# Attention heads in pairs, with products that alternate between halves of the TensorE array

## The chip, the cores and the metric

The kernel runs on one core of one Trainium2 chip. The metric is the device time of one launch in microseconds (us), as the median of several runs. TensorE (PE in the profile) multiplies, VectorE (DVE) and ScalarE (ACT) work on tiles in the two on-chip memories, SBUF and PSUM, GpSimd (POOL) does a few small things, and SyncE (SP) issues the loads.

## The reference, cut to what matters

256 tokens of width 1024 go through two layers of one kind (feed forward, mixer, feed forward) and one block of another (attention, mixture of 32 experts). Attention occurs twice.

- In the mixer of layer 0 there are 4 heads. A head has two queries and two keys of 64 rows each, and values of 128. It subtracts one softmax from the other: `w = probs(qa, k1) - lam * probs(qb, k2)`, and the output is `w @ v`.
- In the last block there are two attentions side by side, each of 8 heads with values of 64 columns. In one (here: moba; with 256 tokens its blocks reduce to plain causal attention) queries and keys have 64 rows, in the other (mla) 64 + 32 = 96.

In each, a score is `q @ k` in 32 bits, scaled and masked causally, and the softmax is taken over the keys.

## The kernel before

Activations lie transposed, features on the 128 partitions and 256 tokens along the columns. Most products are with weights that are split into two float32r parts (`split`: ScalarE's cast on L215, VectorE's subtraction on L216), and three products (`mm3`, L222 to L224) make one full one. Weights come in granules of 1 MB through slots; SyncE's loads are in the order of the program (`dma`, L191), and each waits until its slot is free. The products of attention are plain float32; in the profile such a product is two records of a weight load and a matmul.

A head of attention is a generator, `head` in `mixer0` and `attend` for the last block, with a `yield` between its stages. Stage one: for the first 128 and the last 128 queries (`tt`), the product of queries and keys (128 or 256 columns; L670, L818) into one PSUM bank from the pool `acc` of four, and behind it a bfloat16 product that adds the mask (L672, L819); then VectorE's maxima, ScalarE's exponentials with their sums, VectorE's reciprocal and scaling (L823 to L839). Stage two: three transposes into PSUM (pool `gu` of three; L843) and ScalarE's copy (L845). Stage three: the products with the values (L851 for 256 columns, L852 for 128). Their outputs have 64 partitions, and the halves of a PSUM bank (pool `mi` of one) are filled by an even head and the odd head after it; the odd one also copies the bank out (L855).

`pipeline` lets one head enter a tick; a tick runs one stage of each head under way, the oldest first, and then `n` steps of a generator of fillers. In the last block the fillers are the up projections of mla (six steps for the queries, two for keys and values), eight gates of two steps each, and two parts of an output projection. A step of a projection is 24 `mm3` products. The 16 heads of the last block go through with n = 1, moba's eight first; the four heads of `mixer0` with n = 2. The framework's scheduler orders the instructions of each engine when the program is built, so the order on the chip isn't that of the code in every place; on the chip each engine works strictly through its own list.

Behind the last block's attention come the rest of the output projections and the experts, whose 96 granules are loaded by `moe_fetch` into slots as these come free; the first of these loads are issued during attention.

A product that has no more than 64 rows or 64 output columns is put on a part of the array that follows from the partitions on which its operands and its output start. `gemv_mm` (L266) makes use of that: four products in turn, each writing 32 partitions of one bank.

Of the kernel before, what the change touches and what calls it, by code (L numbers as in the profile page):

```python
# [44 lines left out]
class K:  # L45
# [82 lines left out]
    def pair(self, src0, src1, xH, xL, n, ready=None, inner=True):  # L128
        """Two granules of 256 columns: four PSUM tiles [128, n], side by side (inner) or one after the other."""
# [13 lines left out]
    def gap_fin(self, n, ps):  # L143
        """The product with h, as a tile and a column to be added to it."""
# [23 lines left out]
    def set_ring(self, raw, wsp):  # L168
        """Slots that raw granules and split granules go through, in turn."""
# [19 lines left out]
    def dma(self, dst, src):  # L189
        """Loads are issued in the order of the program."""  # L190
# [4 lines left out]
    def after(self, b, a):  # L195
        """Keeps b behind a in the order of their engine."""
# [4 lines left out]
    def split(self, src, nk, n):  # L201
        """Loads [128, nk*n] and splits it exactly into two float32r parts."""
# [39 lines left out]
    def rows_to_col(self, ps, l, i):  # L242
        """Rows 0, 32, 64, 96 of ps [128, 256] are the quarters of the vector: its columns, plus the bias."""
# [14 lines left out]
    def gemv_mm(self, l, i, ps):  # L258
        """Quarters of c_act @ w_ada[l][:, i] in rows 0, 32, 64, 96 of ps; a granule a step."""
# [16 lines left out]
    def gemv_steps(self, l, i, res):  # L276
        """The same with the products on the vector engine; a granule a step."""
# [24 lines left out]
    def first_cols(self, i, q, col):  # L302
        """Columns 2q, 2q+1 of vector i of layer 0, from the granule of its 256 columns."""
# [24 lines left out]
    def sq_add(self, src, stat):  # L328
        """Takes the squares of src [128, 512] into stat."""
# [6 lines left out]
    def sq_sum(self, stat, lo, hi):  # L336
        """Column sums of pieces lo to hi, [128, 256] each, in four column groups of the array."""
# [22 lines left out]
    def col_sum(self, stat):  # L360
        """Sums over partitions and pieces: [128 tokens, 2] in PSUM."""
# [10 lines left out]
    def bcast(self, rcol, ps=None):  # L372
        """[128 tokens, 2] -> [128, 256] rows, in PSUM."""
# [11 lines left out]
    def h_chunk(self, k, h, rb, a, b, pool=False):  # L385
        """Chunk k of h = x * rstd * a + b, split."""
# [12 lines left out]
    def split_act(self, src, oH, oL):  # L399
        """Splits an SBUF tile."""  # L400
# [4 lines left out]
    def add_res(self, d, srcs, g, stat, nxt=None):  # L405
        """x[2d:2d+2] += g * srcs (PSUM); squares are summed."""
# [13 lines left out]
    def ffn(self, l, j, n, steps, count, ready=None):  # L420
        """n: the operands of gap_begin and gap_end, or h alone with ready, which makes two chunks of h at a time;
        steps: a generator that is advanced once a pair."""
# [72 lines left out]
    def proj_pieces(self, src, nk, cols, xH, xL, evac):  # L495
        """Weights [nk*128, cols] (cols a multiple of 128, up to 256): [128, cols/128, 256] transposed, in PSUM,
        given to evac; a step for each 128 columns."""
# [16 lines left out]
    def tok_pieces(self, src, nk, cols, xH, xL, evac):  # L514
        """Token-major: [128 tokens, 2, cols] in PSUM, given to evac; cols up to 256."""
# [17 lines left out]
    def outproj(self, name, nk, x, g, order=None, nxt=None, then=None):  # L533
        """x(k): the parts of chunk k."""
# [23 lines left out]
    def mixer0(self, n, filler, steps, res):  # L558
# [11 lines left out]
        # statistics over the 64 rows of each component: columns (tt, head, comp)  # L570
# [40 lines left out]
        # lambda  # L611
# [9 lines left out]
        # keys: times rstd over each component  # L621
# [40 lines left out]
        def head(hd):  # L662
            sc = []
            for c in range(2):
                s = self.acc()
                rows = slice(64 * c, 64 * c + 64)
                for tt in range(2):
                    n = P * (tt + 1)
                    o = P * tt
                    nc.tensor.matmul(s[:, o:o + n], qg[rows, hd, tt * P:tt * P + P], kr[rows, hd, :n],  # L670
                                     start=(tt == 0), stop=False, skip_group_check=True)
                    nc.tensor.matmul(s[:, o + n - P:o + n], self.identb, self.maskb,  # L672
                                     start=False, stop=True, skip_group_check=True)
                sc.append(s)
# [25 lines left out]
            # [keys 0, 256 queries | keys 1, 128 queries]  # L700
# [42 lines left out]
    def pipeline(heads, fill, n=1):  # L743
        """Heads enter one a tick; a tick runs one stage of each head under way, the oldest first, and n fillers."""
# [65 lines left out]
    def attend(self, hd, q, k, scol, sconst, vt, out, state):  # L810
        """q, k: [K, 256] slices; scol: [128, 2] query scales or None."""
        nc = self.nc
        s = self.acc()
        offs = (0, P)
        for tt in range(2):
            n = P * (tt + 1)
            o = offs[tt]
            nc.tensor.matmul(s[:, o:o + n], q[:, tt * P:tt * P + P], k[:, :n], start=(tt == 0), stop=False, skip_group_check=True)  # L818
            nc.tensor.matmul(s[:, o + n - P:o + n], self.identb, self.maskb, start=False, stop=True, skip_group_check=True)  # L819
        mx = self.small(2, tag="mx")  # L820
        for tt in range(2):
            n = P * (tt + 1)
            nc.vector.tensor_reduce(mx[:, tt:tt + 1], s[:, offs[tt]:offs[tt] + n], AX.X, ALU.max)  # L823
        nm = self.small(2, tag="nm")
        if scol is None:
            nc.vector.tensor_scalar(nm, mx, -sconst, None, op0=ALU.mult)
        else:
            nc.vector.scalar_tensor_tensor(nm, mx, -1.0, scol, op0=ALU.mult, op1=ALU.mult)
        sm = self.small(2, tag="sum")
        pb = self.pp()  # L830
        for tt in range(2):
            n = P * (tt + 1)
            nc.scalar.activation(pb[:, offs[tt]:offs[tt] + n], s[:, offs[tt]:offs[tt] + n], AF.Exp, bias=nm[:, tt:tt + 1],
                                 scale=sconst if scol is None else scol[:, tt:tt + 1], accum_out=sm[:, tt:tt + 1])
        ri = self.small(2, tag="ri")
        nc.vector.reciprocal(ri, sm)
        for tt in range(2):
            n = P * (tt + 1)
            nc.vector.tensor_scalar(pb[:, offs[tt]:offs[tt] + n], pb[:, offs[tt]:offs[tt] + n], ri[:, tt:tt + 1], None, op0=ALU.mult)  # L839
        yield  # L840
        wt = self.gu()
        for i in range(3):
            nc.tensor.transpose(wt[:, i * P:i * P + P], pb[:, i * P:i * P + P], self.ident)  # L843
# [756 lines left out]
```

## Time and profile before

| | |
|---|---|
| median of 3 runs | 1500.71 us (1499.41 to 1506.01) |
| profiled execution, its span | 1501.8 us; no other time of it is recorded |
| busy, share of the span | PE 95%, PEld 84%, DVE 60%, ACT 43%, POOL 6% |
| DMA | 380.54 MB, mean 253 GB/s |
| first attention | about 278 to 328 us |
| last block's attention | about 1106 to 1204 us |

A line of a timeline gives start, duration, engine, line of the code, operation, `output<-inputs`, the part of the array (rows*columns), the moving operand's size, and how many records in a row are merged. Matmuls are pipelined, so a duration contains a latency that overlaps the next one; the distance from start to start is what one takes up. PEld is the loading of weights. The granted clock (PEclk) is a share of full speed: 1.00 is 2.4 GHz, 0.50 is 1.2 GHz.

### The profile page before, as it was taken

How to read it: one execution, taken by the hardware profiler on the slowest of the kernel's cores; microseconds unless marked ns; L12 is line 12 of the kernel's file. 1: busy time of each engine (PE TensorE's matmuls, PEld its weight loads, DVE VectorE, ACT ScalarE, POOL GpSimd, SP SyncE). 2: the span in 40 equal slices, each digit the busy share in tenths (PEclk: the TensorE clock that was granted, in tenths of full speed). 3: DMA queues.
4: the chain of work that ended last, by engine and by line, in shares of the span. 5: the costliest groups of instructions: out<-in, count | busy, mean ns of one | idle time of the engine just before them, and what ended most of it. 6: DMA issues, size and time to landing. Idle time of an engine off the chain costs nothing. (4 is left out here: it accounts for less than half of the span.)

```text
span 1501.8 us, 27769 instructions
## 1 busy us (share of the span) xinstructions
PE 1423.9 (95%) x11836; PEld 1267.1 (84%) x11837; DVE 900.8 (60%) x1478; ACT 642.2 (43%) x1054; POOL 82.8 (6%) x100
## 2 busy tenths in 40 slices
PE   5999999999999999999999999999999999997775
PEld 3999999879999999999989999999987899554321
DVE  3778757566877759877585685555656555310101
ACT  2444435436444446443463464444536644211011
POOL 0000001111000002000020020000121000000001
PEclk9999999899999999999999999999989999999897
DMA  9888834358778855888655546553434367999996
GB/s 389 301 305 299 295 112 185 123 197 315 273 302 293 300 173 199 312 302 307 209 184 227 196 153 223 215 183 141 173 120 161 121 256 269 379 419 420 420 421 265
DMA packets 53409, 380.54 MB, mean 253 GB/s; under 512 B 5920, under 2 KB 6432, under 8 KB 7712
## 3 DMA queue, kind: packets, MB, share of 16 engines
q1 hardware_dynamic: 53280, 378.71, 66.9%
q8 instruction: 94, 1.54, 0.4%
q14 instruction: 35, 0.29, 0.1%
HBM read 377.64 MB, written 1.05 MB: 252 GB/s over the span
## 5 line engine op out<-in xcount | busy, mean ns | idle before, releaser
L216 DVE TENSOR_TENSOR wl<-raw,wh 128x1024 fp32r<-128x1024 f32 (+2 forms) x381 | 459.9, 1228 | 123.9 <-ACT wh L215 122.4
L215 ACT CAST wh<-raw 128x1024 fp32r<-128x1024 f32 (+2 forms) x381 | 385.8, 1040 | 257.7 <-PE acc L223 88.4
L224 PE MATMUL gu<-hH,wl 128*128 128x256 f32 x1608 | 456.1, 284 | 4.9 <-DVE wl L216 4.7
L222 PE MATMUL gu<-hH,wh 128*128 128x256 f32 x1608 | 458.7, 285 | 1.3 <-ACT t L845 1.1
L223 PE MATMUL gu<-hL,wh 128*128 128x256 f32 x1608 | 455.0, 283 | 0.0
L222 PEld LDWEIGHTS gu<-hH,wh 128*128 128x128 f32 x1608 | 307.4, 191 | 10.7 <-issue 7.2
L224 PEld LDWEIGHTS gu<-hH,wl 128*128 128x128 f32 x1608 | 307.6, 191 | 7.1 <-DVE wl L216 6.9
L223 PEld LDWEIGHTS gu<-hL,wh 128*128 128x128 f32 x1608 | 307.4, 191 | 0.7 <-DVE hL L866 0.4
L222 PE MATMUL acc<-a,wh 128*128 128x256 f32 x704 | 199.3, 283 | 4.9 <-DVE t L149 4.9
L223 PE MATMUL acc<-a,wh 128*128 128x256 f32 x704 | 198.7, 282 | 0.0
L224 PE MATMUL acc<-a,wl 128*128 128x256 f32 x704 | 198.6, 282 | 0.0
L222 PEld LDWEIGHTS acc<-a,wh 128*128 128x128 f32 x704 | 133.2, 189 | 5.4 <-issue 5.4
L223 PEld LDWEIGHTS acc<-a,wh 128*128 128x128 f32 x704 | 133.2, 189 | 0.0
L224 PEld LDWEIGHTS acc<-a,wl 128*128 128x128 f32 x704 | 133.0, 189 | 0.0
L288 DVE SCALAR_TENSOR_TENSOR gacc<-raw,cpad,gacc 128x1024 f32<-128x1024 f32 x91 | 116.6, 1281 | 1.2
L470 ACT ACTIVATE t<-gu 128x256 f32<-128x256 f32 x75 | 28.5, 380 | 144.2 <-PE gu L224 142.3
L1291 PE MATMUL gu<-ex,pp 128*32 128x256 f32 x1024 | 65.4, 399 | 17.3 <-DMA ex<-in_w_exp_up_dram 11.5
L1291 PEld LDWEIGHTS gu<-ex,pp 128*32 128x32 f32 x1024 | 31.7, 113 | 48.3 <-DMA ex<-in_w_exp_up_dram 16.5
L471 DVE TENSOR_TENSOR t<-t,gu 128x256 f32<-128x256 f32 x75 | 31.3, 417 | 64.6 <-ACT t L470 63.4
L402 ACT CAST a<-t 128x256 fp32r<-128x256 f32 x88 | 35.8, 406 | 56.2 <-DVE t L471 38.2
L369 POOL TENSOR_TENSOR sm<-sm,mhalf 128x2 f32<-128x2 f32 (+2 forms) x16 | 18.2, 1138 | 699.1 <-DVE sm L367 665.1
L1304 DVE TENSOR_TENSOR t<-t,gu 128x256 f32<-128x256 f32 x8 | 3.3, 417 | 80.2 <-ACT t L1302 80.2
(350 smaller groups left out, 2110.0 us busy)
## 6 DMA issues: line engine op xcount, KB each, us to landing
raw<-in_w_ada_dram SPq DMA_DIRECT2D x72, 1024.0 KB, 5.1
raw<-in_ffn_wg_dram SPq DMA_DIRECT2D x44, 1024.0 KB, 6.9
raw<-in_ffn_wu_dram SPq DMA_DIRECT2D x44, 1024.0 KB, 7.2
raw<-in_ffn_wd_dram SPq DMA_DIRECT2D x44, 1024.0 KB, 4.9
ex<-in_w_exp_gate_dram SPq DMA_DIRECT2D x32, 1024.0 KB, 19.8
ex<-in_w_exp_up_dram SPq DMA_DIRECT2D x32, 1024.0 KB, 19.8
ex<-in_w_exp_down_dram SPq DMA_DIRECT2D x32, 1024.0 KB, 19.8
raw<-in_w_in_dram SPq DMA_DIRECT2D x18, 1024.0 KB, 4.9
```

The lines of the kernel that those rows point to most:

```text
L215: self.nc.scalar.copy(wh[:, c], r[:, c])
L216: self.nc.vector.tensor_tensor(wl[:, c], r[:, c], wh[:, c].bitcast(F32), op=ALU.subtract)
L222: mm(out, wh, xh, start=start, stop=False, skip_group_check=True)
L223: mm(out, wh, xl, start=False, stop=False, skip_group_check=True)
L224: mm(out, wl, xh, start=False, stop=stop, skip_group_check=True)
L288: d = nc.vector.scalar_tensor_tensor(acc, g[:, kk, :], c, acc, op0=ALU.mult, op1=ALU.add)
L369: self.pow = nc.gpsimd.tensor_tensor(r, ms, self.mhalf[:, :w], op=ALU.pow)
L402: nc.scalar.copy(oH, src)
L470: nc.scalar.activation(s, pg, AF.Silu)
L471: nc.vector.tensor_tensor(a, s, pu, op=ALU.mult)
L1291: nc.tensor.matmul(ps[32 * e:32 * e + 32, z * T:z * T + T], xg[:, k * P + 32 * e:k * P + 32 * e + 32], w[:, e, kk, :], start=(k == 0), sto ...
L1304: nc.vector.tensor_tensor(a, s, ps[:, T:], op=ALU.mult)
```

## The change

Scores get a helper, `scores`, which both kinds of attention call: it issues the four products of a pair first (for each `tt`, one of z = 0, one of z = 1) and the four masks behind them. In `mixer0` the pair is the two components of a head; the rest of `head` stays. `attend` now takes two heads, `c` and `z`, through all of its stages: two `acc` tiles of scores, one `pp` tile for both weights, one tile of two for each small vector of four columns, transposes of z = 0 in a `gu` tile and of z = 1 in an `acc` tile, and products with values that alternate between partitions 0 to 63 and 64 to 127 of one `mi` tile. The last block has 8 pairs and `pipeline` takes two fillers a tick. Comments and docstrings go too.

```diff
         def head(hd):
-            sc = []
-            for c in range(2):
-                s = self.acc()
-                rows = slice(64 * c, 64 * c + 64)
-                for tt in range(2):
-                    n = P * (tt + 1)
-                    o = P * tt
-                    nc.tensor.matmul(s[:, o:o + n], qg[rows, hd, tt * P:tt * P + P], kr[rows, hd, :n],
-                                     start=(tt == 0), stop=False, skip_group_check=True)
-                    nc.tensor.matmul(s[:, o + n - P:o + n], self.identb, self.maskb,
-                                     start=False, stop=True, skip_group_check=True)
-                sc.append(s)
+            sc = [self.acc(), self.acc()]
+            self.scores(sc, [qg[64 * c:64 * c + 64, hd, :] for c in range(2)], [kr[64 * c:64 * c + 64, hd, :] for c in range(2)])
...
-    def attend(self, hd, q, k, scol, sconst, vt, out, state):
+    def scores(self, sc, qs, ks):
         nc = self.nc
-        s = self.acc()
-        offs = (0, P)
         for tt in range(2):
-            n = P * (tt + 1)
-            o = offs[tt]
-            nc.tensor.matmul(s[:, o:o + n], q[:, tt * P:tt * P + P], k[:, :n], start=(tt == 0), stop=False, skip_group_check=True)
-            nc.tensor.matmul(s[:, o + n - P:o + n], self.identb, self.maskb, start=False, stop=True, skip_group_check=True)
+            n, o = P * (tt + 1), P * tt
+            for z in range(2):
+                nc.tensor.matmul(sc[z][:, o:o + n], qs[z][:, tt * P:tt * P + P], ks[z][:, :n],
+                                 start=(tt == 0), stop=False, skip_group_check=True)
+        for z in range(2):
+            for tt in range(2):
+                o = P * tt + P * tt
+                nc.tensor.matmul(sc[z][:, o:o + P], self.identb, self.maskb, start=False, stop=True, skip_group_check=True)
+
+    def attend(self, c, qs, ks, scol, sconst, vt, out):
+        nc = self.nc
+        sc = [self.acc(), self.acc()]
+        self.scores(sc, qs, ks)
...
+        ws = []
+        for z in range(2):
+            wt = self.acc() if z else self.gu()
+            for i in range(3):
+                nc.tensor.transpose(wt[:, i * P:i * P + P], pb[:, 384 * z + i * P:384 * z + i * P + P], self.ident)
+            w = self.t2()
+            nc.scalar.copy(w[:, :384], wt[:, :384])
+            ws.append(w)
         yield
-        if hd % 2 == 0:
-            state["po"] = self.mi()
-        po = state["po"]
-        r = slice(64 * (hd % 2), 64 * (hd % 2) + 64)
-        nc.tensor.matmul(po[r, :T], vt[:, 0, hd * 64:hd * 64 + 64], ws[:, :T], start=True, stop=False, skip_group_check=True)
-        nc.tensor.matmul(po[r, P:T], vt[:, 1, hd * 64:hd * 64 + 64], ws[:, T:T + P], start=False, stop=True, skip_group_check=True)
-        if hd % 2 == 1:
-            c = hd // 2
-            nc.scalar.copy(out[:, c, :], po[:, :T])
+        po = self.mi()
+        for i, (cols, r) in enumerate(((slice(0, T), slice(0, T)), (slice(P, T), slice(T, T + P)))):
+            for z in range(2):
+                hd = 2 * c + z
+                nc.tensor.matmul(po[64 * z:64 * z + 64, cols], vt[:, i, hd * 64:hd * 64 + 64], ws[z][:, r],
+                                 start=(i == 0), stop=(i == 1), skip_group_check=True)
+        nc.scalar.copy(out[:, c, :], po[:, :T])
         yield
...
-        for hd in range(8):
-            r = slice(64 * (hd % 2), 64 * (hd % 2) + 64)
-            heads.append(self.attend(hd, qb[r, hd // 2, :], kb[r, hd // 2, :], None, 0.125, v2(vb), ob, stt))
-        for hd in range(8):
-            heads.append(self.attend(hd, Q[hd // 4][0:96, hd % 4, :], Kt[hd // 4][0:96, hd % 4, :], scq, None, v2(vm), oa, stt))
+        for c in range(4):
+            rows = (slice(0, 64), slice(64, P))
+            heads.append(self.attend(c, [qb[r, c, :] for r in rows], [kb[r, c, :] for r in rows], None, 0.125, v2(vb), ob))
+        for c in range(4):
+            qk = [[t[c // 2][0:96, (2 * c + z) % 4, :] for z in range(2)] for t in (Q, Kt)]
+            heads.append(self.attend(c, *qk, scq, None, v2(vm), oa))
         fill = chain()
-        self.pipeline(heads, fill)
+        self.pipeline(heads, fill, 2)
```

The middle of `attend`, cut here, does for z = 0 and z = 1 what it did for one head: four maxima, one operation that makes the four offsets, four exponentials, and for each z one reciprocal and two scalings.

## Rows read from the trace of the kernel before

**Rows 1.** The page: busy time of each engine, share of the span, instructions.

```profile
PE 1423.9 (95%) x11836; PEld 1267.1 (84%) x11837; DVE 900.8 (60%) x1478; ACT 642.2 (43%) x1054; POOL 82.8 (6%) x100
```

**Rows 2.** Windows: length, busy us (count) by engine, clock, DMA share, GB/s.

```profile
280.00:300.00 20.00, 20.00 (x122) 15.03 (x120) 12.84 (x40) 11.84 (x32) 0.00 (x0) 0.83 0.14 52
310.00:330.00 20.00, 17.18 (x135) 11.66 (x134) 15.39 (x46) 6.96 (x16) 3.26 (x14) 0.91 0.57 211
1106.00:1120.00 14.00, 14.00 (x69) 11.45 (x69) 6.64 (x15) 3.42 (x8) 4.62 (x4) 0.63 0.33 112
1106.00:1206.00 100.00, 98.93 (x667) 83.42 (x667) 59.40 (x146) 58.54 (x133) 10.68 (x12) 0.95 0.40 140
1266.00:1476.00 210.00, 176.01 (x1712) 94.50 (x1712) 30.18 (x106) 32.61 (x93) 0.70 (x1) 0.93 0.99 409
```

**Rows 3.** Longest waits: PE, 1120 to 1206 us; SP, 1090 to 1500 (total, times, longest).

```profile
PE gu L222 <- ACT t L845: 1.1, 1, 1.1
...
SPq L191 <- DVE wl L216: 112.1, 18, 11.8
```

**Rows 4.** Timeline of PE, a moba head's products with values.

```profile
1147.01 0.28 PE L224 MATMUL gu<-cqH,wl 128*128 128x256 f32 x1
1147.22 0.65 PE L851 MATMUL mi<-t,m 128*64 128x256 f32 x2
1147.70 0.38 PE L852 MATMUL mi<-t,m 128*64 128x128 f32 x2
1148.01 0.55 PE L843 MATMUL gu<-cst,pp 128*128 128x128 f32 x3
```

**Rows 5.** Timeline of PE, products that write quarters of a bank in turn.

```profile
313.04 1.93 PE L266 MATMUL gu<-raw,cpad 128*32 128x256 f32 x30
```

**Rows 6.** Timeline of PE, scores of `mixer0`, one component of a head and the next.

```profile
285.93 0.49 PE L670 MATMUL acc<-m 64*128 64x128 f32 x2
286.35 0.23 PE L672 MATMUL acc<-bt 128*128 128x128 bf16 x1
286.50 0.70 PE L670 MATMUL acc<-m 64*128 64x256 f32 x2
287.13 0.23 PE L672 MATMUL acc<-bt 128*128 128x128 bf16 x1
287.29 0.54 PE L670 MATMUL acc<-m 64*128 64x128 f32 x1
```

**Rows 7.** Timeline of PE, scores of mla heads.

```profile
1154.85 0.44 PE L818 MATMUL acc<-m,m 96*128 96x128 f32 x2
1155.12 0.22 PE L819 MATMUL acc<-bt 128*128 128x128 bf16 x1
1155.18 0.65 PE L818 MATMUL acc<-m,m 96*128 96x256 f32 x2
1155.67 0.22 PE L819 MATMUL acc<-bt 128*128 128x128 bf16 x1
1155.73 0.44 PE L818 MATMUL acc<-m,m 96*128 96x128 f32 x2
...
1179.32 0.39 PE L818 MATMUL acc<-m,m 96*128 96x128 f32 x2
1179.54 0.22 PE L819 MATMUL acc<-bt 128*128 128x128 bf16 x1
```

**Rows 8.** Groups by line, 1120 to 1206 us: busy, mean ns | idle before, releaser.

```profile
L216 DVE TENSOR_TENSOR wl<-raw,wh 128x1024 fp32r<-128x1024 f32 (+1 forms) x20 | 22.5, 1142 | 8.4 <-ACT wh L215 8.3
L823 DVE TENSOR_REDUCE sm<-acc 128x1 f32<-128x128 f32 (+1 forms) x28 | 8.9, 352 | 10.8 <-PE acc L819 10.7
L839 DVE TENSOR_SCALAR pp<-pp,sm 128x128 f32<-128x128 f32 (+1 forms) x32 | 8.9, 319 | 0.6
...
L833 ACT ACTIVATE pp<-acc,sm,sm 128x128 f32<-128x128 f32 (+1 forms) x16 | 8.1, 511 | 3.3 <-DVE sm L828 2.8 <-DVE sm L836 0.4
...
L833 ACT ACTIVATION_READ_ACCUMULATOR pp<-acc,sm,sm 128x1 f32 x16 | 3.2, 200 | 0.0
```

More of the change, by code (lines that the diff above doesn't have):

```diff
@@ L807, in mixer1 @@
         return mixH, mixL
-    def attend(self, hd, q, k, scol, sconst, vt, out, state):
+    def scores(self, sc, qs, ks):
         nc = self.nc
-        s = self.acc()
-        offs = (0, P)
         for tt in range(2):
-            n = P * (tt + 1)
-            o = offs[tt]
-            nc.tensor.matmul(s[:, o:o + n], q[:, tt * P:tt * P + P], k[:, :n], start=(tt == 0), stop=False, skip_group_check=True)
-            nc.tensor.matmul(s[:, o + n - P:o + n], self.identb, self.maskb, start=False, stop=True, skip_group_check=True)
[L820 to L824, printed above, removed]
+            n, o = P * (tt + 1), P * tt
[10 more added lines that the diff above has]
+        self.scores(sc, qs, ks)
+        part = [slice(0, P), slice(P, 3 * P)]
+        mx = self.small(4, tag="mx")
+        for z in range(2):
+            for tt in range(2):
+                nc.vector.tensor_reduce(mx[:, 2 * z + tt:2 * z + tt + 1], sc[z][:, part[tt]], AX.X, ALU.max)
+        nm = self.small(4, tag="nm")
         if scol is None:
@@ L827, in attend @@
         else:
-            nc.vector.scalar_tensor_tensor(nm, mx, -1.0, scol, op0=ALU.mult, op1=ALU.mult)
-        sm = self.small(2, tag="sum")
+            v = lambda t: t.rearrange("p (z t) -> p z t", z=2)
+            nc.vector.scalar_tensor_tensor(v(nm), v(mx), -1.0, scol.unsqueeze(1).to_broadcast([P, 2, 2]), op0=ALU.mult, op1=ALU.mult)
+        sm = self.small(4, tag="sum")
         pb = self.pp()
[L831 to L839, printed above, removed]
-        yield
-        wt = self.gu()
-        for i in range(3):
-            nc.tensor.transpose(wt[:, i * P:i * P + P], pb[:, i * P:i * P + P], self.ident)
-        ws = self.t2()
-        nc.scalar.copy(ws[:, :384], wt[:, :384])
@@ L846, in attend @@
-        yield
-        if hd % 2 == 0:
-            state["po"] = self.mi()
-        po = state["po"]
-        r = slice(64 * (hd % 2), 64 * (hd % 2) + 64)
-        nc.tensor.matmul(po[r, :T], vt[:, 0, hd * 64:hd * 64 + 64], ws[:, :T], start=True, stop=False, skip_group_check=True)
-        nc.tensor.matmul(po[r, P:T], vt[:, 1, hd * 64:hd * 64 + 64], ws[:, T:T + P], start=False, stop=True, skip_group_check=True)
-        if hd % 2 == 1:
-            c = hd // 2
-            nc.scalar.copy(out[:, c, :], po[:, :T])
+        ri = self.small(4, tag="ri")
@@ new lines, in attend @@
+        for z in range(2):
+            p = pb[:, 384 * z:384 * z + 384]
+            for tt in range(2):
+                i = 2 * z + tt
+                nc.scalar.activation(p[:, part[tt]], sc[z][:, part[tt]], AF.Exp, bias=nm[:, i:i + 1],
+                                     scale=sconst if scol is None else scol[:, tt:tt + 1], accum_out=sm[:, i:i + 1])
+        for z in range(2):
+            p = pb[:, 384 * z:384 * z + 384]
+            nc.vector.reciprocal(ri[:, 2 * z:2 * z + 2], sm[:, 2 * z:2 * z + 2])
+            for tt in range(2):
+                i = 2 * z + tt
+                nc.vector.tensor_scalar(p[:, part[tt]], p[:, part[tt]], ri[:, i:i + 1], None, op0=ALU.mult)
@@ new lines, in attend @@
+        yield
+        ws = []
+        for z in range(2):
+            wt = self.acc() if z else self.gu()
[4 more added lines that the diff above has]
+            ws.append(w)
+        yield
+        po = self.mi()
+        for i, (cols, r) in enumerate(((slice(0, T), slice(0, T)), (slice(P, T), slice(T, T + P)))):
+            for z in range(2):
+                hd = 2 * c + z
+                nc.tensor.matmul(po[64 * z:64 * z + 64, cols], vt[:, i, hd * 64:hd * 64 + 64], ws[z][:, r],
+                                 start=(i == 0), stop=(i == 1), skip_group_check=True)
@@ L1066, in block2 @@
         v2 = lambda t: t.rearrange("p (t a) b -> p t (a b)", t=2)
-        stt = {}
         heads = []
-        for hd in range(8):
-            r = slice(64 * (hd % 2), 64 * (hd % 2) + 64)
-            heads.append(self.attend(hd, qb[r, hd // 2, :], kb[r, hd // 2, :], None, 0.125, v2(vb), ob, stt))
-        for hd in range(8):
-            heads.append(self.attend(hd, Q[hd // 4][0:96, hd % 4, :], Kt[hd // 4][0:96, hd % 4, :], scq, None, v2(vm), oa, stt))
+        for c in range(4):
[4 more added lines that the diff above has]
+            heads.append(self.attend(c, *qk, scq, None, v2(vm), oa))
         fill = chain()
-        self.pipeline(heads, fill)
+        self.pipeline(heads, fill, 2)
         for _ in fill:
```

## The prediction

> **What bounds the kernel now.** I read the page first [rows 1]: TensorE is busy 95% of the span, so wherever it is never idle, TensorE is the engine to shorten. That is an average, so I then took the stretches around the edit [rows 2]. In the second attention stage (1106 to 1206 us) PE is busy 98.9 of 100 us, VectorE 59.4 and ScalarE 58.5, DMA at 0.40 of its engines: work taken off PE there shortens the stretch, as long as the other two can follow. In the first attention stage PE is busy all of 280 to 300 us, but 17.2 of the 20 us from 310 to 330, in its tail. The waits [rows 3] agree: over 86 us of the second stage the longest PE wait is one of 1.1 us, for ScalarE's copy of the transposed weights.
>
> From 1266 us on the DMA engines are the bound: 0.99 of their time at 409 GB/s, PE 84%. Does time saved before that reach the end? In the second attention stage the share is 0.40, so bandwidth is free, and SyncE's longest waits are for the splits that read a weight slot empty [rows 3]. The loads that fill the experts' slots are held by compute. If compute reaches 1266 earlier by S, the slots come free S earlier, as many bytes remain, and the saturated stretch shifts by S as a whole. So I count upstream savings in full.
>
> **Products over values (every pair of heads of the second stage).** Before, a head issues two products of 64 output columns, alone. [rows 4]: the last full product starts at 1147.01, L851 at 1147.22 (0.21 where full products follow each other by 0.12, so 0.09 for going into the 64-column form), L852 at 1147.70, the next full one at 1148.01: 0.79 + 0.09 = 0.88 a head, 1.76 a pair. After, head z writes partitions 64z to 64z+63, and the products alternate between the halves. The kernel already has products that alternate between quarters of the columns, L266 [rows 5]: 30 records in 1.93 us, 0.064 each, where one 256-column record of L851 holds the engine for 0.24 (0.48 for two). So quarters run side by side, and I take the halves to: a pair costs what one head did, 0.88. 8 pairs x 0.88 = 7.0 us saved. If they didn't overlap, only one way in and out is saved: 8 x 0.18 = 1.4.
>
> **Scores of 64 rows (4 heads of the first stage, 4 pairs of the second).** Before, every product of 64 rows is followed by a mask product of 128 rows. [rows 6]: 285.93 to 287.29 is one half, 1.36 us, 2.72 for both: 0.42 for the product of 128 columns, 0.63 for 256, and 0.15 from each mask to the next product. With 96 rows the same steps take 0.27, 0.49 and 0.06 [rows 7], so a 64-row product pays some 0.15 more and its return some 0.09 more. After, the four products stand together, alternating between rows 0 to 63 and 64 to 127, each half in a PSUM tile of its own, and the four masks follow. One half's products in line: 0.42 + 0.63 = 1.05; entry 0.10; masks 4 x 0.06 = 0.24; 1.39 if the halves overlap wholly. No row of before shows two halves of the rows in flight; the nearest is L266 with its column quarters. I take overlap, and 0.1 for the second half running behind: 1.5, so 1.2 saved a pair, 8 x 1.2 = 9.6 us. Ends: whole overlap 8 x 1.33 = 10.6; none, 2 x 1.05 + 0.34 = 2.44, 8 x 0.28 = 2.2.
>
> **Scores of 96 rows (4 pairs).** These fill more than half of the rows and can't run side by side. A head takes 0.88 (1154.85 to 1155.73 [rows 7]), a pair 1.76. After, only the first product of a pair follows a mask; the same product behind a 32-bit one takes 0.22 instead of 0.27 (1179.32 [rows 7]), and I count twice that, 0.44, for 256 columns: 2 x 0.66 + 0.05 + 4 x 0.06 = 1.61. 4 x 0.15 = 0.6; at worst nothing.
>
> **The clock.** The granted clock is 0.83 in 280 to 300 us and 0.63 in 1106 to 1120 [rows 2]: part of each ran at the lower level, 1.2 GHz. Before the first fall TensorE ran score products, head behind head [rows 6]. Worked as lost time: 20 x 0.17 = 3.4 and 14 x 0.37 = 5.2. Shorter, fuller runs of scores may shorten these stretches; the second may not. Between 0 and 8.6, I take 2.
>
> **What else moves.** ScalarE's exponentials, copies and output copies, and VectorE's maxima, reciprocals and scalings keep their number; 8 small VectorE operations (L826, L828) go, off the path. Fillers go two to a tick of a pair, 16 heads x 1 against 8 pairs x 2, and the first 96-row pair enters behind eight fillers as its head did. No DMA is added or moved past another. PSUM: a pair takes two tiles of the four-deep pool for scores and a third for its second transposes; the other transposes keep one of three.
>
> **New waits.** From scores to transposes a pair now needs [rows 8]: four maxima 4 x 0.35 = 1.4, four exponentials with their sums read 4 x 0.71 = 2.8, two scalings 0.6, and between them two operations on 2 to 4 columns, each at most a maximum, 0.4 together: 5.2 us; 7.4 with a split of 1.1 queued ahead on VectorE and its cast, of as many columns, on ScalarE. Cover: two fillers of 24 products at 0.12, 5.8, and a pair's value products, 0.9: 6.7. If late, transposes wait, and behind them in PE's queue the value products and fillers. That is 0 to 0.7 a pair, 0 to 6; I take 2. In the first stage the end (310 to 330 us) has 2.8 us in which PE waits on other engines; some of the saving ends there: 1 us.
>
> **Sum.** 7.0 + 9.6 + 0.6 + 2 - 2 - 1 = 16.2. The profiled execution's span is 1501.8, all that is known of its time, which gives 1485.6; the median of the runs is 1.1 below that span, so 1484.5, a gain of 1.1%.
>
> **A rule weighed.** Alternating quarters of the columns take 0.064 a record where one alone takes 0.24 [rows 4, 5], a quarter: all four are in flight at once. The Trainium skill, "TensorE: Matmul & The Clock Gate", Part 3, says that products start and end strictly in order of issue. A 32-bit product here is two records, so by that rule one half's first pass could start no earlier than the other half's second; L266 would then take 0.12 a record, and the trace speaks against it, for columns. By the rows the sum is 16.2, by the rule 3.5 less (the first rival).
>
> **Rivals.**
> - The two passes of a 32-bit product go before the other half's first, in order. A pass of 128 columns takes 0.11 (half of 0.22 [rows 7]), one of 256 0.22. A pair's value products, 0.66 with both halves in step, become 0.88, since each second half starts a pass late; 0.22 a pair, and I count the same for the scores. 16 x 0.22 = 3.5 less gain: 1488.0. For it: halves of the rows are unseen. Against it: [rows 5].
> - Halves of the rows don't overlap at all: 2.2 instead of 9.6, gain 8.8, time 1491.9. For it: a 64-row pass seems to wait for its weights (0.63 against 0.49 for 256 columns). Against it: the other half could load meanwhile.
> - The work comes off PE, but ScalarE and VectorE, at 59% of a stretch that shrinks by an eighth, become late: 1 us a pair more, 8 us back, 1492.5 to 1495.
> - The written order isn't the executed one: the scheduler moves instructions, and the scores of two heads stand back to back at 1154.85 and 1155.73 [rows 7] although the code puts a filler between heads. If the products don't alternate, 1.4 + 2.2 + 0.6 less 2 of waits: 1498.5.
> - Slower: a pair's softmax holds up PE. Its price is what 5.2 to 7.4 us grows to over 6.7. To undo the 18.2 us gained without waits it needs 2.3 us a pair, to be seen 3.2, a chain of 9.9 us. At 3.5, 28 us, it ends at 1510.5. Against it: today's equivalent, half as much work under half as much cover, leaves 1.1 us of waits in 86.
>
> **How the numbers follow.** Forecast as worked 0.57; strict order 0.15; no overlap of rows 0.10; late ScalarE and VectorE 0.10; not alternating 0.04; slower 0.04. The measurement tells 0.5%, 7.5 us, from no change, so "faster" is below 1493.2: 0.57 + 0.15 + 0.07 (no overlap of rows) + 0.04 (late engines) = 0.83; the other 0.03 of no overlap, 0.06 of late engines and 0.04 of not alternating make "same" 0.13; "slower" 0.04. Range: from everything at its best end, 7.0 + 10.6 + 0.6 + 8.6 = 26.8 gained, 1474, to the late engines' 1495.
>
> **What would show it.** Right: in a pair, the two L851-type products start within some hundredths of each other and the pair takes 0.9, not 1.76; scores of a 64-row pair from first product to last mask take 1.5, not 2.7; the second attention stage is shorter by some 10 us and the first by 4 to 6; the stretch from 1266 us on keeps its length. Wrong: second products of the halves start behind the first one's end; PE waits of several us for ScalarE's copy or VectorE's scaling; a longer stretch of low clock; the DMA-bound end growing by what was saved.

## The result and the profile after

The change takes 1480.7 us (median of 4 runs, 1480.33 to 1482.13), beside 1503.1 us of the kernel before (4 runs: the three known before and one of 1505.5): a ratio of 0.9851, 95% interval [0.9832, 0.9871]. That is faster by 22 us; 16 were forecast. The profiled execution's span went from 1501.8 to 1478.5 us.

The page of the changed kernel, busy time by engine, as in [rows 1]:

```profile
PE 1398.9 (95%) x11836; PEld 1251.0 (85%) x11837; DVE 898.9 (61%) x1470; ACT 641.1 (43%) x1054; POOL 81.7 (6%) x100
```

TensorE lost 25.0 us of busy time with the same 11836 products, and the span lost 23.3: nearly all that came off the busiest engine arrived at the end. The windows of [rows 2] again; the last three columns are granted clock, DMA share, GB/s:

```profile
280.00:300.00 20.00, 19.72 (x161) 16.23 (x161) 15.39 (x50) 15.14 (x44) 0.80 (x2) 1.00 0.41 162
310.00:330.00 20.00, 18.49 (x138) 16.14 (x139) 14.09 (x31) 9.31 (x15) 0.99 (x4) 0.91 0.41 150
1106.00:1120.00 14.00, 12.74 (x106) 11.79 (x106) 8.47 (x18) 10.95 (x24) 0.00 (x0) 1.00 0.39 138
1106.00:1206.00 100.00, 97.68 (x793) 89.07 (x792) 67.14 (x142) 67.11 (x142) 6.28 (x8) 1.00 0.50 182
1266.00:1476.00 210.00, 168.41 (x1586) 81.54 (x1576) 27.86 (x68) 30.15 (x86) 4.86 (x5) 0.90 0.95 392
```

In 280 to 300 and 1106 to 1120 us TensorE starts 161 and 106 products where it started 122 and 69, at a clock of 1.00 where it had 0.83 and 0.63. VectorE and ScalarE rose from 59 to 67 of 100 us and still follow. In the last window the loads now end before 1476, as the DMA-bound stretch begins and ends earlier.

TensorE's timeline of a 64-row pair (scores, masks, the next full product), then of a pair's value products and, behind two sets of transposes, a 96-row pair:

```profile
1115.05 0.93 PE L807 MATMUL acc<-m 64*128 64x128 f32 x8
1115.90 0.40 PE L812 MATMUL acc<-bt 128*128 128x128 bf16 x4
1116.11 0.36 PE L222 MATMUL gu<-cqH,wh 128*128 128x256 f32 x1
...
1147.23 0.28 PE L224 MATMUL gu<-hH,wl 128*128 128x256 f32 x1
1147.44 0.87 PE L860 MATMUL mi<-t,m 128*64 128x256 f32 x8
1148.24 0.55 PE L851 MATMUL gu<-cst,pp 128*128 128x128 f32 x3
...
1148.96 1.48 PE L807 MATMUL acc<-m,m 96*128 96x128 f32 x8
1150.27 0.39 PE L812 MATMUL acc<-bt 128*128 128x128 bf16 x4
1150.47 0.36 PE L222 MATMUL gu<-hH,wh 128*128 128x256 f32 x1
```

From start to start: the eight passes of four 64-row products take 0.85, the four masks 0.21, together 1.06 where [rows 6] give 2.72. The value products of a pair take 0.80, plus 0.09 for entering (1147.23 to 1147.44 instead of 0.12), where two heads took 1.76 [rows 4]. A 96-row pair takes 1.51, not 1.76 [rows 7]. In the trace the two halves' first passes start 7 ns apart, 0.007 of 0.85 us: they run side by side.

TensorE's waits from 1096 to 1185 us, to hold against [rows 3] (total, times, longest):

```profile
PE gu L224 <- DVE wl L216: 0.8, 1, 0.8
PE gu L851 <- DVE pp L845: 0.5, 1, 0.5
PE gu L222 <- ACT wh L215: 0.5, 1, 0.5
PE gu L222 <- ACT t L853: 0.2, 1, 0.2
PE gu L222 <- DVE m L997: 0.2, 1, 0.2
```

2.2 us over these 89 us, one each: the softmax of a pair is late for its transposes (L851) once, by 0.5.

To place the gain I cut each trace at the same four lines of the code: the first product of `mixer0`'s lambda (L616) to the last product of its pooling (L650), and the last block's first statistics (L356) to its first router product. "Low" is the time at 1.2 GHz inside the two stages, from the granted clock's stretches. All in us:

| kernel | ahead | first stage | between | second stage | rest | span | low, first + second |
|---|---|---|---|---|---|---|---|
| before | 273.3 | 54.3 | 725.4 | 206.4 | 242.4 | 1501.8 | 14.0 + 10.2 |
| before, again | 273.8 | 54.3 | 726.4 | 206.4 | 241.2 | 1502.2 | 11.9 + 10.2 |
| after | 271.2 | 45.1 | 727.1 | 191.5 | 243.6 | 1478.5 | 5.7 + 0 |
| after, again | 270.9 | 46.4 | 728.1 | 191.4 | 243.0 | 1479.7 | 8.8 + 0 |

The first stage is shorter by 8 to 9 us and the second by 15. The other three parts moved by 1 to 3 us each, two up and one down, and together by less than 1. So the rest, in which the loads are the bound, kept its length, and what was saved ahead of it arrived.

### The profile page after: what moved, and what is told of

The parts are those of the page before. It is cut to its first block, busy times and chain, and to the rows that moved or that the text cites. A ratio compares the mean times of both kernels' runs of the same rounds, so it can differ in the third digit from the quotient of the medians.

```text
span 1478.5 us, 27754 instructions
## 1 busy us (share of the span) xinstructions
PE 1398.9 (95%) x11836; PEld 1251.0 (85%) x11837; DVE 898.9 (61%) x1470; ACT 641.1 (43%) x1054; POOL 81.7 (6%) x100
## 3 DMA queue, kind: packets, MB, share of 16 engines
HBM read 377.64 MB, written 1.05 MB: 256 GB/s over the span
## 5 line engine op out<-in xcount | busy, mean ns | idle before, releaser
L1298 PE MATMUL gu<-ex,pp 128*32 128x256 f32 x1024 | 67.2, 408 | 14.9 <-DMA ex<-in_w_exp_up_dram 9.7
```

The source lines that it names most:

```text
L1298: nc.tensor.matmul(ps[32 * e:32 * e + 32, z * T:z * T + T], xg[:, k * P + 32 * e:k * P + 32 * e + 32], w[:, e, kk, :], start=(k == 0), sto ...
```

## Experiments

The theory behind them: the gain comes from products of two halves of the array in flight together, for scores by rows and for values by columns. The main rivals: that it is the order alone (alternating), the regrouping alone (fewer changes of form between 64-row and full products), or the clock.

**One part alone: the first stage.** The kernel before, with `mixer0` calling the new `scores`; the last block stays.

```diff
-            sc = []
-            for c in range(2):
...
+            sc = [self.acc(), self.acc()]
+            self.scores(sc, [qg[64 * c:64 * c + 64, hd, :] for c in range(2)], [kr[64 * c:64 * c + 64, hd, :] for c in range(2)])
```

> The kernel before, with the first attention stage's scores alone put into the new order (four products alternating between the halves of the rows, then four masks); the last block keeps one head at a time. Theory (the rows' halves run side by side, and the time of PE is what counts): the trace of after has a pair's four products in 0.86 us where the kernel before takes 2.72 with masks, and 1.84 where one half had to wait; with masks a pair saves about 1.5, three pairs of four in full: 4 x 1.5 - 1 = 5, plus up to 3 of clock that fell behind the long run of scores: 5 to 8 us faster than before, ratio 0.9947 to 0.9967. Rival (the tail of the stage, in which PE waits for VectorE, takes it back): less than 3 us, ratio above 0.998.

Measured: 1495.8 us, 0.9948 [0.9934, 0.9962] of before, 8 us less. The first stage lasts 45.9 us, the second 203.6. The four heads of the first stage hold half of the 64-row work (4 of 8 pairs) and bring 8 of the 22 us. Not all of the profiled gain is theirs: the second stage, whose code is as before, is 2.8 us shorter in this execution, with 3.4 us at 1.2 GHz where the kernel before has 10.2.

**One part alone: pairs without grouped scores.** Each 64-row product is followed by its mask again, and the value products are listed half by half.

```diff
-        for tt in range(2):
-            n, o = P * (tt + 1), P * tt
-            for z in range(2):
+        for z in range(2):
+            for tt in range(2):
+                n, o = P * (tt + 1), P * tt
                 nc.tensor.matmul(sc[z][:, o:o + n], ...)
-        for z in range(2):
-            for tt in range(2):
-                o = P * tt + P * tt
-                nc.tensor.matmul(sc[z][:, o:o + P], self.identb, self.maskb, ...)
+                nc.tensor.matmul(sc[z][:, o + n - P:o + n], self.identb, self.maskb, ...)
...
-        for i, (cols, r) in enumerate(...):
-            for z in range(2):
+        for z in range(2):
+            for i, (cols, r) in enumerate(...):
```

> The changed kernel with its pairs, tiles and two fillers a tick, but no alternation: scores as product, mask, product, mask for one half and then the other, value products of one half and then of the other. Theory (the gain is overlap and fewer changes of form): only one way in and out of the 64-column form a pair is saved, 1.4 us, less some waits: within 4 us of the kernel before, ratio 0.997 to 1.003. Rival (the pairs themselves, with longer stretches of fillers and fewer small steps, bring a good part): 8 us or more of the 22 stay, ratio below 0.995.

Measured: 1496.8 us, 0.9964 [0.995, 0.9978]: 5.4 us less than before, more than I expected. One reason stands in TensorE's timeline of this kernel:

```profile
1132.26 0.88 PE L857 MATMUL mi<-t,m 128*64 128x256 f32 x8
1133.07 0.55 PE L848 MATMUL gu<-cst,pp 128*128 128x128 f32 x3
```

A pair's value products take 0.81 though listed half by half. The overlap did not need the alternating order, so this run holds the value products' part and isn't a base without it. The clock is the other reason: in the profile, of the fastest of its seven runs, the first stage is as long as before (54.5 us), and the second lasts 195.0 instead of 206.4, with no time at 1.2 GHz instead of 10.2 us. From 195.0 to the change's 191.5, that is 3.5 us, is what the grouped scores of the last block bring.

**Undoing the alternation, scores and values apart.** In the first run the `scores` loop has `z` outside `tt`, masks behind all four; in the second the value loop has `z` outside.

```diff
-        for tt in range(2):
-            n, o = P * (tt + 1), P * tt
-            for z in range(2):
+        for z in range(2):
+            for tt in range(2):
+                n, o = P * (tt + 1), P * tt
```

> The changed kernel with the four score products of a pair in the order of halves (both of one half, then both of the other), the masks still behind all four; instruction lists of all other engines stay the same. Theory (side by side only if the halves alternate, as the next product of the same half blocks the list): a pair goes from 0.86 us to 1.5 at 8 pairs, about 5 us slower than the changed kernel: ratio to before about 0.988 to 0.990. Rival (what counts is that the products stand together, free of changes of form; or each half has a queue of its own and overlaps in any order): less than 1 us, ratio as the changed kernel's, 0.985.

> The changed kernel with a pair's value products in the order of halves of the columns (both of one head, then both of the other); all other lists stay the same. Theory: a pair goes from 0.80 us to 1.2 or 1.3, since only the neighbours at the seam overlap: 8 x 0.45 = 3.6 us slower than the changed kernel, ratio to before 0.987 to 0.988. Rival (queues by half, any order overlaps): 0.80 us a pair, no change.

Measured: 1481.9 us, 0.9855 [0.984, 0.9869], and 1480.8 us, 0.9858 [0.9842, 0.9875]: both the change's own time. TensorE's timeline of the first:

```profile
1117.84 0.93 PE L807 MATMUL acc<-m 64*128 64x128 f32 x8
1118.70 0.40 PE L812 MATMUL acc<-bt 128*128 128x128 bf16 x4
```

Eight passes in 0.86, as with alternation. By the records' own starts the second half begins 13 ns after the first, ahead of three passes of the first half that precede it in the list (the scheduler kept the written order: in the list it built for TensorE, every pair of this run has both products of one half before the other's). So with four passes a half the order doesn't matter; what is needed is that the products stand together. The Trainium skill, "TensorE: Matmul & The Clock Gate", says that matmuls start strictly in the order of issue (Part 3). This trace disagrees: three passes that stand earlier in the list start later. The sentence under "The kernel before" that each engine works strictly through its own list is wrong for TensorE too.

**Taking the overlap away, grouping kept.** Both halves on the same half of the array: first for scores (the second component's scores are computed from rows 0 to 63), then for values (both heads' outputs on partitions 0 to 63, with one copy more per pair, to bring the second to its place).

```diff
-            self.scores(sc, [qg[64 * c:64 * c + 64, hd, :] for c in range(2)], ...)
+            self.scores(sc, [qg[0:64, hd, :] for c in range(2)], ...)
...
-            rows = (slice(0, 64), slice(64, P))
+            rows = (slice(0, 64), slice(0, 64))
```
```diff
-                nc.tensor.matmul(po[64 * z:64 * z + 64, cols], ...)
-        nc.scalar.copy(out[:, c, :], po[:, :T])
+                nc.tensor.matmul(po[0:64, z * T + lo:z * T + T], ...)
+        for z in range(2):
+            nc.scalar.copy(out[64 * z:64 * z + 64, c, :], po[0:64, z * T:z * T + T])
```

> The changed kernel, in which the second score pair of every 64-row pair is computed from the rows 0 to 63 too (so the second head or component uses the first one's queries and keys); all instruction lists stay the same, only the rows on which these products stand. It tells overlap from standing together. Theory (overlap of the halves of the rows): the four products run one after the other without a change of form, about 0.86 + 0.65 = 1.5 us instead of 0.86: 8 x 0.65 = 5 us slower than the changed kernel, ratio to before about 0.9885. Rival (standing together is enough): no change, 0.985.

> The changed kernel, in which both heads of a pair write their values' products to partitions 0 to 63, in two halves of the bank's columns, and two copies bring them out. Theory (overlap of the halves of the columns): a pair's value products take 0.80 + 0.64 = 1.44 us instead of 0.80, 8 x 0.64 = 5 us slower, and one more small copy of ScalarE's a pair, beside other work: ratio to before about 0.988 to 0.989. Rival: no change, 0.985.

Measured: 1483.8 us, 0.9881 [0.9864, 0.9897], and 1489.4 us, 0.9899 [0.9882, 0.9917]. Timelines of the two, scores of a 64-row pair in the first, value products in the second:

```profile
1117.77 1.57 PE L807 MATMUL acc<-m 64*128 64x128 f32 x8
1119.27 0.40 PE L812 MATMUL acc<-bt 128*128 128x128 bf16 x4
```
```profile
1124.05 1.51 PE L860 MATMUL mi<-t,m 128*64 128x256 f32 x8
1125.50 0.55 PE L851 MATMUL gu<-cst,pp 128*128 128x128 f32 x3
```

Scores 1.50 instead of 0.85, values 1.45 instead of 0.80: 0.65 a pair each is the overlap itself, 5.2 us over eight pairs. By the ratios the runs cost 0.0030 and 0.0048, 4.5 and 7.2 us; the second has the further copies too.

**Full products between the halves.** The two products of a half, its two masks, then the other half (the diff is against the scores listed by half).

```diff
         for z in range(2):
             for tt in range(2):
                 n, o = P * (tt + 1), P * tt
                 nc.tensor.matmul(sc[z][:, o:o + n], ...)
-        for z in range(2):
             for tt in range(2):
                 o = P * tt + P * tt
                 nc.tensor.matmul(sc[z][:, o:o + P], self.identb, self.maskb, ...)
```

> The changed kernel with scores as: both products of one half, its two masks, both products of the other half, its two masks. Half of the changes of form of the old order, and full-array masks stand between the halves, so no overlap. Theory: a pair takes 0.1 + 0.86 + 0.11 + 0.15 + 0.86 + 0.11 = 2.2 us with masks, where the old order takes 2.72 and the changed one some 1.2: ratio to before 0.990 to 0.992, that is about 8 us slower than the changed kernel and 4 faster than the pairs without alternation. Rival (TensorE looks past the masks): 0.985.

Measured: 1488.0 us, 0.99 [0.9885, 0.9915]. Timeline:

```profile
1121.45 0.92 PE L807 MATMUL acc<-m 64*128 64x128 f32 x4
1122.30 0.28 PE L811 MATMUL acc<-bt 128*128 128x128 bf16 x2
1122.51 0.92 PE L807 MATMUL acc<-m 64*128 64x128 f32 x4
1123.37 0.28 PE L811 MATMUL acc<-bt 128*128 128x128 bf16 x2
1123.46 0.36 PE L222 MATMUL gu<-cqH,wh 128*128 128x256 f32 x1
```

1.06 for the first half and 0.95 for the second, 2.01 a pair: the products of one half alone take as long (0.85) as those of both together. Masks that use the whole array keep the halves apart. So a 64-row pair with its masks, and a full product behind it, comes down in three steps: 2.61 with a mask behind each product (1125.17 to 1127.78 in the pairs without grouped scores; [rows 6] give 2.72 where another 64-row product follows), 2.01 by halves, 1.71 with all four together on the same rows (1.50 + 0.21), 1.06 on different rows.

In the last block not all of this arrives. With both halves on the same rows the second stage is longer by 1.0 us than the change's, not by 4 x 0.65 = 2.6, and with masks between by 1.7, not by 4 x 0.95 = 3.8. In the change TensorE waits there for a split, a cast and a pair's scaling (0.8 + 0.5 + 0.5 us, in the waits above); with both halves on the same rows only the 0.8 of these is left.

**A try to do better.** One head of the first stage, which the scheduler lists by half, waits between its halves for a PSUM bank, in TensorE's timeline of the changed kernel:

```profile
282.02 1.91 PE L807 MATMUL acc<-m 64*128 64x128 f32 x8
283.86 0.40 PE L812 MATMUL acc<-bt 128*128 128x128 bf16 x4
```

1.84 instead of 0.85. The second component's scores were put into the other pool.

```diff
-            sc = [self.acc(), self.acc()]
+            sc = [self.acc(), self.gu()]
```

> An attempt at more: the changed kernel, with the second component's scores of the first stage in a bank of the pool of three instead of the pool of four, because in the changed kernel's trace one of its four heads waits for a fourth free bank and runs its halves one after the other (1.84 us instead of 0.86). If all four overlap: about 1 us faster than the changed kernel, ratio 0.9845, at the edge of what can be told; if the fillers now wait for the pool of three instead, 0 to 3 us slower.

Measured: 1488.8 us, 0.9908 [0.9893, 0.9923], 8 us slower than the change. With other banks the scheduler placed the start of the stage elsewhere. TensorE's largest wait there, and two windows, of this kernel; then the same windows of the change:

```profile
PE mi L629 <- DVE t L624: 4.0, 2, 2.4
...
262.00:272.00 10.00, 6.76 (x59) 5.52 (x57) 3.13 (x5) 5.32 (x7) 5.93 (x2) 0.81 0.76 288
272.00:282.00 10.00, 7.55 (x49) 6.22 (x50) 5.54 (x14) 1.80 (x7) 0.75 (x1) 0.68 0.29 105
```
```profile
262.00:272.00 10.00, 10.00 (x86) 9.27 (x86) 3.14 (x5) 5.26 (x7) 4.46 (x2) 0.91 0.81 306
272.00:282.00 10.00, 9.04 (x68) 6.99 (x66) 6.27 (x17) 2.37 (x7) 2.21 (x1) 0.92 0.39 136
```

TensorE is idle 5.7 us of these 20, waiting above all for VectorE (L624), and has 0.81 and 0.68 of its clock where the change has 0.91 and 0.92. A wait of 1 us was traded for one of 4 and a slower clock.

**Is it the clock?** Both kernels again, for second profiles.

> The kernel before once more, for a second profile. Theory (the old order of scores brings the clock's falls in the two stages): TensorE's granted clock is at 1.2 GHz again within a few us of 287 us and of 1106 us from the start of the span, and the stages last about 54 and 206 us as in the first profile. Rival (those falls were a chance of one execution): one or both are missing, and the stages are shorter by half the time of the falls that are missing, 3 us and 5 us.

> The change once more, for a second profile. Theory: no fall near 287 us nor near 1106 us, stages of about 45 and 191.5 us. Rival: a fall of 3 to 10 us at one of them, with a stage longer by half of it.

Measured: 1504.4 and 1481.7 us, beside one run of before on that chip at 1501.2. Windows over the two stages of the kernel before, then of the change:

```profile
273.80:328.10 54.30, 50.55 (x344) 37.97 (x344) 33.97 (x101) 22.30 (x59) 6.84 (x17) 0.89 0.44 166
1054.50:1260.90 206.40, 203.83 (x1536) 185.93 (x1535) 131.95 (x259) 109.13 (x197) 19.48 (x22) 0.98 0.49 177
```
```profile
270.90:317.30 46.40, 42.73 (x336) 33.59 (x335) 33.07 (x101) 21.48 (x58) 7.07 (x17) 0.91 0.52 195
1045.40:1236.80 191.40, 187.54 (x1538) 175.87 (x1536) 131.13 (x251) 108.21 (x198) 19.65 (x22) 1.00 0.52 190
```

The stretches at 1.2 GHz came back: before has them again from 289.2 us (3.4 us) and from 1108.4 (10.2), the change has neither. So they aren't the chance of one execution; the length of the first differs (6.8 and 3.4 us). Over all fourteen traces of this study: near 1106 us the clock fell in the three with single heads (10.2, 10.2 and, in the first experiment, 3.4 us) and in none of the eleven with pairs, not even with the old order of scores. Near 287 it fell in five, before (twice), the second experiment and the two runs below, all with slow scores in the first stage, and not in the other nine. That slow scores bring that fall isn't shown: scores on the same rows (1.50 a pair) had none, and the last run (1.49) had one.

**How far TensorE looks ahead.** The 64-row products are cut to 64 columns, so a half has twelve passes, not four; listed half by half, then alternating (the second diff is against the first).

```diff
+        w = 64 if qs[0].shape[0] <= 64 else 2 * P
+        for z in range(2):
+            for tt in range(2):
+                n, o = P * (tt + 1), P * tt
+                for lo in range(0, n, w):
+                    hi = min(lo + w, n)
+                    nc.tensor.matmul(sc[z][:, o + lo:o + hi], qs[z][:, tt * P:tt * P + P], ks[z][:, lo:hi], ...)
```
```diff
-        for z in range(2):
-            for tt in range(2):
-                n, o = P * (tt + 1), P * tt
-                for lo in range(0, n, w):
-                    hi = min(lo + w, n)
+        for tt in range(2):
+            n, o = P * (tt + 1), P * tt
+            for lo in range(0, n, w):
+                hi = min(lo + w, n)
+                for z in range(2):
```

> The change with the four 64-row score products of a pair listed half by half and each cut into products of 64 columns, so that 12 passes of the one half stand in the list before the first pass of the other. Theory (TensorE starts products of a free half of the array ahead of those of a busy half, however many stand between): the second half starts within about 0.1 us of the first, and the 12 products of a pair last 0.9 to 1.3 us; time within 4 us of the change's. Rival (it looks ahead by a few products only, and four passes were within that): the second half starts when most of the first is through, the 12 products last 1.5 to 2.2 us, and over 8 pairs the kernel is 4 to 9 us slower than the change, about 1485 to 1490 us.

> The kernel of the experiment before with one thing changed: the products of 64 columns alternate between the halves of the rows. In the run before, the second half of a pair began 0.95 us after the first, when nine of the first half's twelve passes had started, and the 24 passes of a pair lasted about 2.45 us at the full clock. Theory (TensorE looks ahead by only a few passes, about four, so the order in the list decides once a half has more passes than that): both halves start within 0.02 us of each other, the passes start every 0.056 us, and a pair lasts 1.4 to 1.6 us; over 8 pairs that is some 8 us less than the run before, about 1486 us. Rival (products of 64 columns do not overlap well whatever their order, because the loading of their weights sets the pace): a pair stays at 2.2 to 2.5 us and the time at about 1494 us.

Measured: 1494.4 and 1486.6 us. Timelines of the two:

```profile
1109.00 2.50 PE L810 MATMUL acc<-m 64*128 64x64 f32 x24
1111.43 0.40 PE L815 MATMUL acc<-bt 128*128 128x128 bf16 x4
```
```profile
1102.83 1.56 PE L810 MATMUL acc<-m 64*128 64x64 f32 x24
1104.32 0.40 PE L815 MATMUL acc<-bt 128*128 128x128 bf16 x4
```

2.43 by half, 1.49 alternating. The records' own starts in the first (us, one pair; the first pass of a half is the one that lasts 0.320):

```
first half   1108.998 1109.158 .270 .381 .493 .605 .716 .828 .940 | three more
second half  1109.946 1110.106 .217 ...
```

The second half begins when nine of the first half's twelve passes have started and three have not. With four passes a half it began when one had started and three had not. In one head of this run's first stage, where fillers leave six passes of the first half in the block, it began when three had started (304.933, 305.093, 305.204, then the second half at 305.210). All three cases say that TensorE reaches past three waiting passes and no further (my reading of them). Here, past four passes a half, the alternating order matters: 0.94 us in each of the six pairs that stand in one block. The two times differ by 7.8 us, but they are single runs on two chips, on which single runs of the kernel before took 1501.2 and 1507.4; the pace in the traces is the evidence.

## Why the prediction was right, and where it was off

The mechanism held at each step; the gain, 16.2 forecast and some 22 measured, was short mainly by one term, the clock. Counted in the profiled executions, from each TensorE instruction's start to the next one's, at the full clock except where the clock is the subject; each figure is good to some tenths. What the lower clock costs stands in the timeline of the kernel before, where full products follow each other by 0.213 us at 1.2 GHz and, 5 us later, by 0.120 at 2.4 GHz:

```profile
1114.37 0.41 PE L224 MATMUL gu<-wh,hL 128*128 128x256 f32 x1
1114.58 0.41 PE L222 MATMUL gu<-wh,hH 128*128 128x256 f32 x1
...
1118.90 0.28 PE L224 MATMUL gu<-wh,hL 128*128 128x256 f32 x1
1119.02 0.28 PE L222 MATMUL gu<-wh,hH 128*128 128x256 f32 x1
```

The terms one by one:

- **Value products, 7.0:** 5.4. A pair takes the 0.80 and 0.09 that were forecast where it stands alone. One pair is split by fillers into two blocks, and TensorE idles 0.7 us at two of the pairs. The pairs without grouped scores are also faster by 5.4 [3.3, 7.5], the ratio's interval times 1503, but as the clock's fall is gone in their profile too, that run isn't a measure of this term alone.
- **Scores of 64 rows, 9.6:** 10.0 (products and masks took 20.7 before and 10.7 after), by two errors that nearly cancel. "One half's products in line: 0.42 + 0.63 = 1.05" took prices from products that come behind a mask [rows 6]; in one block only the first pass pays for that, a half takes 0.85, the second half runs 7 ns behind and not 0.1 us, and a full pair saves 1.66, not 1.22. But 8 x 1.66 = 13.3 isn't reached: two of the first stage's heads lose 1.9 us (one waits 1.0 for its bank, one is cut in two, and a full product stands among the masks), and a pair of the last block cost some 0.2 less than 2.72 before, because a mask that a full product follows holds TensorE for less than one that a 64-row product follows.
- **Scores of 96 rows, 0.6:** 0.8.
- **The clock, "between 0 and 8.6, I take 2":** 6 to 8. This is the step that failed. By the two spacings above 0.44 of the time at 1.2 GHz is lost (1 - 0.120 / 0.213; an estimate, as not all of that time holds such products): 0.44 x (14.0 + 10.2 - 5.7) = 8.1 in the first profiles, 0.44 x (11.9 + 10.2 - 8.8) = 5.8 in the second. I took a quarter of what [rows 2] showed; both falls that stand there went as a whole.
- **Waits, -2, and the first stage's tail, -1:** the terms above add up to 5.4 + 10.0 + 0.8 + 8.1 = 24.3 in the first profiles and, with 5.8, to 22.0 in the second, where the stages became shorter by 24.1 (9.2 + 14.9) and 22.9 (7.9 + 15.0). In total that agrees within 1 us, by stage it doesn't. The second stage is shorter by 15 where its terms give 5.4 + 5.7 + 0.8 + 4.5 = 16.4, so some 1.4 went to waits, near the 2 that I took off. The first is shorter by 9.2 and 7.9 where scores and clock give 4.3 + 3.6 = 7.9 and 4.3 + 1.4 = 5.7: the 1 for its tail doesn't show, and where the further 1 to 2 us come from stays open. The cover of 6.7 us for a pair's softmax was enough in all cases but one.
- **What would show it:** the first stage was to be shorter by 4 to 6 us and the second by some 10; they are by 8 to 9 and 15. The DMA-bound end kept its length.

Of the rivals, the strict order of passes (1488.0) is refuted by passes that start ahead of earlier ones. Halves of rows that don't overlap (1491.9): they do, and without it the kernel takes 1483.8, so I had priced that rival's loss, 7.4 us, too high; the measured one is 4.5 by the ratios, whose intervals reach 2 to 3 us to either side. Late engines and a slow softmax (1492.5 and up) didn't come: VectorE and ScalarE, at 67%, keep up. That the products wouldn't alternate (1498.5) took the alternation for the cause; the runs by half show that with four passes a half it is worth nothing. Standing in one block is what counts: masks between the halves cost 7 us.

What stays open is what brings the clock's falls. The one near 1106 us went with the single heads in all fourteen traces, but no run isolates what it is about them, so 6 to 8 of the 22 us are measured and not explained.

## What to carry to other kernels

Products that use only half of the array's rows or columns should stand in one block, on both halves, with nothing that uses the whole array between them; where a half has more than some four passes, list them alternately. Price a product inside such a block by the ones inside a block, not by one that comes behind a change of form. Where a granted clock under 1 covers the stretch that a change shortens, give that loss a term of its own, up to the whole of it: here it was a quarter to a third of the gain.

## What the runs showed of the hardware

- TensorE starts matmuls out of the order of its list: passes on a free half of the array go ahead of up to three waiting passes of the busy half (13 ns behind its first pass; 0.95 us with twelve passes a half).
- Passes of 64 columns start every 0.112 us in a half, as do those of 128 (1115.259 to 1115.371 in the changed kernel, 0.112): a pass of 64 columns was no cheaper than one of 128. That fits the alternating version with cut products, where a pair takes 1.49 instead of 0.85 (one run, 1486.6 us).
- Two full-array masks between the halves ended the overlap: 2.01 us a pair, 1.06 without them. The Trainium skill, "TensorEngine Tiling (Array Packing)", Key Properties, says that changing the tiling mode drains TensorE; the trace fits that, with 0.09 to 0.10 us more between starts at entry (1147.23 to 1147.44) and 0.21 instead of 0.11 for the first pass of 128 columns.
